# Low parts of sixteen weight blocks: a subtraction on VectorE replaced by a second ScalarE copy and an accumulating SBUF-to-SBUF transfer

## The chip, the cores and the metric

The kernel runs on one core of a Trainium2 chip, as one launch. The metric is device time in microseconds (us). The engines are TensorE (PE in the profile; PEld is its weight load), VectorE (DVE), ScalarE (ACT), GpSimd (POOL) and SyncE (SP, which here only issues DMA transfers). Each runs its own instructions in order and waits for others by semaphores. Sixteen DMA engines move the data of all queues.

## The reference, cut to what matters

One inference step of a decoder layer on 512 prompt positions and 8 x 4 sample positions (544 rows of 1024 channels). A wide input projection feeds three branches (mLSTM, spatial gating, RG-LRU), each is gated, projected and merged, then comes an output projection and a layer norm. The change touches the weights of two of the fifteen parts of the input projection, z_b and u_b:

```python
proj = jnp.einsum('btd,de->bte', x, p['w_in']) + p['b_in']
(q, k, v_a, o_a, z_a, i_pre, f_pre, u_b, v_b, z_b, x_c, z_c,
 g_a, g_b, g_c) = jnp.split(proj, _split_points(), axis=-1)
...
vn = layer_norm(v_b, p['gmlp_ln_g'], p['gmlp_ln_b'])
y_b = chunk_spatial_gate(u_b, vn, p['gmlp_ws'], p['gmlp_bs']) * jax.nn.silu(z_b)
```

All data is float32.

## The kernel before

**Split products.** A float32 product is made from three TensorE products of rounded numbers (type float32r): each operand is split into a high part (the rounded value) and a low part (what is left), and high x high, high x low and low x high are added in PSUM. For x the parts are xh and xl, held in SBUF for the whole run, transposed (8 tiles of 128 channels x 544 rows). For weights they are made block by block.

**Units.** The work on TensorE is a list of tasks, each 128 output columns of one weight matrix: names like zb0 to zb7 and u0 to u7. For a plain task `project` (L414) runs one unit: 8 contraction steps k, each with 3 x 2 products of 128x272 (`products`, L349): first two with (wh, xh), then two with (wh, xl), then two with (wl, xh). So wl is read from the fifth product of a unit on. The task zb0 takes the steps in the order 4 to 7, then 0 to 3. The vb pairs just before zb0 go through `seven` (L360), a scheme with seven products of half blocks.

**Weights.** `load` (L262) fetches raw weights for two neighbouring tasks (256 columns, 1 MB, two SP transfers) into one of two raw buffers. `need` (L274) makes wh and wl of one task from it: ScalarE writes wh = raw, rounded to float32r (L286), then VectorE writes wl = raw - wh (L287). wh and wl have three buffers each. `prep(n+2)` is called at step k = 1 of unit n, so the parts of a unit are made two units ahead. For zb0 and zb1 that call stands inside `seven` of the last vb pair, in its third and fourth part.

**Order.** The program order of TensorE, ScalarE, VectorE and GpSimd is as written; side work (generators: `norm_v`, `mixers`) is put between products by a clock that counts the TensorE work issued so far. Around the first zb units there are also: the restore of eight pieces of xh and xl from DRAM (`restore`, L497, by SP), the loads of the layer-norm rows (L1366, L1367), the transposes and the layer norm of v (`norm_v`, L1361), and `mixers` (L1303), whose affine_select (L1310) and the power of the layer norm (L1354) run on GpSimd. Ahead of each u unit TensorE makes the mix products (`pre_u`, L1286). Results of a unit are taken from PSUM by ScalarE (L758, L759 for zb) and VectorE.

**Accumulating transfers before.** GpSimd issues twenty transfers that add 256 KB of raw weights from DRAM onto SBUF (`block`, L253, with onto), for the tasks that go through `seven`, mostly two in a row: one onto a raw buffer (wr), one onto s3 (shown as s).

Of the kernel before, what the change touches and what calls it, by code (L numbers as in the profile page):

```python
# [11 lines left out]
AF = mybir.ActivationFunctionType  # L12
ALU = mybir.AluOpType
PSUM = bass.MemoryType.PSUM

P = 128
# [25 lines left out]
def kernel(  # L42
# [6 lines left out]
    nc = tc.nc  # L49
    ET = mybir.EngineType  # L50
    ctx.enter_context(tc.manual_schedule(engines={ET.PE, ET.Activation, ET.DVE, ET.Pool}))
    V, A, G, PE = nc.vector, nc.scalar, nc.gpsimd, nc.tensor
# [33 lines left out]
    def f(ap):  # L86
        return ap.bitcast(F32)
# [174 lines left out]
    def load(i):  # L262
        name, w2d, off, c, *_ = tasks[i]
        c0 = off - c * P
        if (id(w2d), c0) not in raws:
            raws[id(w2d), c0] = raw = sp.tile([P, KT, 256], F32, tag="wraw", name=f"wr_{name}", bufs=2)
            for q in range(0, KT, 4):
                nc.sync.dma_start(raw[:, q:q + 4, :], w2d[q * P:(q + 4) * P, c0:c0 + 256].rearrange("(k p) c -> p k c", p=P))
            if name in fast:

                block(raw[:, 0:4, P:2 * P], i, 1, 1, True)
        return raws[id(w2d), c0]

    def need(i, parts=1):  # L274
        if i >= len(tasks) or i in wts:
            return
        name, w2d, off, c, *_ = tasks[i]
        raw = load(i)
        wh = sp.tile([P, KT, P], F32R, tag="wh", name=f"wh_{name}", bufs=3)
        wl = sp.tile([P, KT, P], F32R, tag="wl", name=f"wl_{name}", bufs=3)  # L280
        wts[i] = (wh, wl)
        n = KT // parts
        for q in range(parts):
            ks = slice(q * n, q * n + n)
            src = raw[:, ks, c * P:(c + 1) * P]
            A.activation(wh[:, ks, :], src, AF.Copy)  # L286
            V.tensor_tensor(wl[:, ks, :], src, f(wh[:, ks, :]), op=ALU.subtract)  # L287
            yield
# [48 lines left out]
    def prep(n, whole=True):  # L337
        if n >= len(seq):
            return
        if n not in preps:  # L340
            i, q = seq[n]
            preps[n] = need(i) if q is None else factors(i, q)
        if whole:
            for _ in preps[n]:
                pass
        else:
            next(preps[n], None)
# [189 lines left out]

    def start():
        w0, w1 = need(0, 4), need(1, 4)

        warm = m2("warm")
# [15 lines left out]
        xps[1] = x_rows(1)  # L557
        heat(3)
        w2 = need(2, 2)
        for k in range(KT):  # L560
            if k + 1 < KT:
# [183 lines left out]
    ya, yc, zb, yb = {}, {}, {}, {}  # L745
# [867 lines left out]
```

## Time and profile before

| | us |
|---|---|
| median of 3 runs | 980.22 (977.94 to 981.2) |
| the profiled execution | 978.44 |
| its span, from the first to the last instruction | 976.4 |
| TensorE busy | 959.8 |
| VectorE busy | 613.3 |
| ScalarE busy | 447.9 |
| GpSimd busy | 123.4 |

The profile is of one execution. Its page gives busy times and the chain of work that ended last; the trace behind it answers for a stretch, an engine or a tile. Times within the span count from its start. An instruction line gives its start, its duration, the engine, the line of the kernel, and what it writes and reads (`out<-in`); an x4 merges four like instructions. In brackets stands the idle time of the engine ahead of it and what ended that. "Landing" is the time from a transfer's issue to its completion.

### The profile page before, as it was taken

The page shows a single profiled execution, that of the slowest core. Times are in us where ns is not written, and L with a number is a line of the kernel's source. Part 1 is how long each engine was busy: PE and PEld are TensorE (multiplying, and loading weights), DVE is VectorE, ACT ScalarE, POOL GpSimd, SP SyncE. Part 2 cuts the span into 40 slices and gives each one's busy share as a digit, 9 for nine tenths or more (in the row PEclk, how much of TensorE's full clock was granted, in tenths as well). Part 3 has the DMA queues.
Part 4 walks back from the last instruction along what each step waited for, and adds up shares of the span by engine and source line. Part 5 has one row for each costly group of instructions (what it writes and reads, how often), then busy time and mean ns, then how long its engine had stood idle before and what let it go on. Part 6 is the DMA issues. An engine that isn't in the chain of part 4 may idle for free.

```text
span 976.4 us, 17919 instructions
## 1 busy us (share of the span) xinstructions
PE 959.8 (98%) x7313; PEld 934.2 (96%) x7313; DVE 613.3 (63%) x1033; ACT 447.9 (46%) x747; POOL 123.4 (13%) x230
## 2 busy tenths in 40 slices
PE   9999999999999999999999999999999999999996
PEld 8999999999999999999999999999999999999975
DVE  4665675566567568889987465556677455433456
ACT  4454445445444544889935353334433213322411
POOL 5122101200210120001111111112000000000204
PEclk9999999999999999999999999999999999999999
DMA  9333622541362252332153755557633222430322
GB/s 300 104 63 120 218 66 77 177 149 44 121 217 74 74 165 85 98 97 78 59 131 90 143 136 129 119 137 161 179 118 114 87 92 76 142 113 34 103 66 102
DMA packets 120113, 113.64 MB, mean 116 GB/s; under 512 B 6094, under 2 KB 113464, under 8 KB 120032
## 3 DMA queue, kind: packets, MB, share of 16 engines
q1 hardware_dynamic: 107936, 106.31, 34.8%
q0 software_dynamic: 11456, 5.55, 4.9%
q8 instruction: 57, 0.93, 0.4%
q10 hardware_dynamic: 640, 0.66, 0.2%
q14 instruction: 24, 0.20, 0.1%
HBM read 99.38 MB, written 13.11 MB: 115 GB/s over the span
## 4 chain that ended last, share of the span: by engine, by line
PE 89%; DVE 5%; ACT 2%; DMA 1%; issue 1%; POOL 0%; POOLq 0%; DVEq 0%; ACTq 0%
PE out L103 5%; PE ps_v L103 5%; PE ps_zc L103 5%; PE ps_u L103 5%; PE ps_z L103 5%; PE ps_q L103 5%; PE ps_zb L103 5%; PE ps_xc L103 5%; PE ps_pb L103 5%; PE ps_o L103 5%; PE ps_k L103 5%; PE ps_pc L103 5%; PE ps_gb L103 5%; PE ps_pa L103 2%; PE px_gc L103 2%; PE sc L103 2%
## 5 line engine op out<-in xcount | busy, mean ns | idle before, releaser
L993 DVE SCALAR_TENSOR_TENSOR c<-c,bc,cs 128x512 f32<-128x512 f32 x32 | 23.9, 747 | 36.2 <-PE cs L103 35.8
L975 POOL TENSOR_SCALAR wvm<-wvt,bm 96x256 fp32r<-96x256 f32 x32 | 31.5, 987 | 87.4 <-PE cs L103 87.4
L103 PE MATMUL ps_v<-xh,wh_v 128*128 128x272 f32 x128 | 28.4, 305 | 0.0
L972 ACT ACTIVATE c0h<-c 128x512 fp32r<-128x512 f32 x32 | 20.0, 625 | 17.2 <-DMA c<-in_state_mlstm_c_dram 8.8
L103 PE MATMUL ps_v<-xh,wl_v 128*128 128x272 f32 x128 | 27.4, 296 | 0.0
L103 PE MATMUL ps_u<-xh,wh_u 128*128 128x272 f32 x128 | 27.3, 295 | 0.0
L103 PE MATMUL ps_q<-xh,wh_q 128*128 128x272 f32 x128 | 27.3, 294 | 0.0
L103 PE MATMUL ps_v<-xl,wh_v 128*128 128x272 f32 x128 | 27.3, 295 | 0.0
L103 PE MATMUL ps_zc<-xh,wh_zc 128*128 128x272 f32 x128 | 27.2, 295 | 0.0
L103 PE MATMUL ps_o<-xl,wh_o 128*128 128x272 f32 x128 | 27.2, 293 | 0.0
L103 PE MATMUL ps_zc<-xl,wh_zc 128*128 128x272 f32 x128 | 27.1, 294 | 0.0
L103 PE MATMUL ps_zc<-xh,wl_zc 128*128 128x272 f32 x128 | 27.0, 293 | 0.0
L103 PE MATMUL ps_zb<-xh,wl_zb 128*128 128x272 f32 x128 | 27.0, 292 | 0.0
L103 PE MATMUL ps_z<-xh,wl_z 128*128 128x272 f32 x128 | 26.9, 291 | 0.0
L103 PE MATMUL ps_o<-xh,wl_o 128*128 128x272 f32 x128 | 26.8, 291 | 0.0
L103 PE MATMUL ps_z<-xh,wh_z 128*128 128x272 f32 x128 | 26.7, 290 | 0.0
L103 PE MATMUL ps_q<-xl,wh_q 128*128 128x272 f32 x128 | 26.7, 289 | 0.0
L103 PE MATMUL ps_q<-xh,wl_q 128*128 128x272 f32 x128 | 26.7, 290 | 0.0
L103 PE MATMUL ps_zb<-xl,wh_zb 128*128 128x272 f32 x128 | 26.6, 289 | 0.0
L103 PE MATMUL ps_zb<-xh,wh_zb 128*128 128x272 f32 x128 | 26.6, 289 | 0.0
L103 PE MATMUL ps_xc<-xl,wh_xc 128*128 128x272 f32 x128 | 26.6, 289 | 0.0
L103 PE MATMUL ps_k<-xh,wl_k 128*128 128x272 f32 x128 | 26.6, 289 | 0.0
(905 smaller groups left out, 3471.3 us busy)
## 6 DMA issues: line engine op xcount, KB each, us to landing
c<-in_state_mlstm_c_dram SPq DMA_DIRECT2D x32, 256.0 KB
out_dram<-c SPq DMA_DIRECT2D x32, 256.0 KB
wr_q<-in_w_in_dram SPq DMA_DIRECT2D x8, 512.0 KB
wr_k<-in_w_in_dram SPq DMA_DIRECT2D x8, 512.0 KB
wr_o<-in_w_in_dram SPq DMA_DIRECT2D x8, 512.0 KB
wr_z<-in_w_in_dram SPq DMA_DIRECT2D x8, 512.0 KB
wr_xc<-in_w_in_dram SPq DMA_DIRECT2D x8, 512.0 KB
wr_zc<-in_w_in_dram SPq DMA_DIRECT2D x8, 512.0 KB
```

Of the source, the lines that this page charges most:

```text
L103: PE.matmul(out, a, b, start=start, stop=stop, skip_group_check=more)
L972: A.activation(hi[:, :512], t_[:, :512], AF.Copy)
L975: G.tensor_scalar(wvm, f(wvs), bm[:, b:b + 1], None, op0=ALU.mult)
L993: V.scalar_tensor_tensor(t_[:, :512], t_[:, :512], inter[:, DS * b + DS - 1:DS * b + DS], ps, op0=ALU.mult, op1=ALU.add)
```

## The change

For the tasks zb0 to zb7 and u0 to u7 the low part is made in another way. ScalarE writes wh as before, for all 8 steps in one instruction, and then writes wl = -raw, rounded in the same way, that is -wh. Then GpSimd issues a transfer from SBUF to SBUF that adds the raw weights onto wl (512 KB, in pieces of 128 numbers, since raw holds the columns of two tasks). wl is then raw - wh. VectorE has no part in it, and the raw buffer is read last by that transfer. All other tasks stay as they were.

```diff
@@ -279,6 +279,14 @@
         wh = sp.tile([P, KT, P], F32R, tag="wh", name=f"wh_{name}", bufs=3)
         wl = sp.tile([P, KT, P], F32R, tag="wl", name=f"wl_{name}", bufs=3)
         wts[i] = (wh, wl)
+        if name[:-1] in ("zb", "u"):
+
+            src = raw[:, :, c * P:(c + 1) * P]
+            A.activation(wh, src, AF.Copy)
+            A.activation(wl, src, AF.Copy, scale=-1.0)
+            nc.gpsimd.dma_start(f(wl), src, accum_op=ALU.add)
+            yield
+            return
         n = KT // parts
         for q in range(parts):
             ks = slice(q * n, q * n + n)
```

## Rows read from the trace of the kernel before

**Rows 1.** The page: busy time, share of the span and number of instructions of each engine; then the chain that ended last, its shares of the span by engine.
```profile
PE 959.8 (98%) x7313; PEld 934.2 (96%) x7313; DVE 613.3 (63%) x1033; ACT 447.9 (46%) x747; POOL 123.4 (13%) x230
...
PE 89%; DVE 5%; ACT 2%; DMA 1%; issue 1%; POOL 0%; POOLq 0%; DVEq 0%; ACTq 0%
```

**Rows 2.** The waits of TensorE over the whole span, longest first: who waited for whom, us in total, times, the longest.
```profile
PE px_ga L103 <- ACT gta L370: 1.5, 1, 1.5
```

**Rows 3.** Busy time by windows, the stretch of the zb units and that of the u units: window, its length, busy us of each engine with the number of instructions, the granted clock of TensorE, the share of the DMA engines, GB/s.
```profile
702.10:760.00 57.90, 57.90 (x467) 57.18 (x467) 39.57 (x63) 20.14 (x28) 3.24 (x6) 1.00 0.44 137
760.00:820.00 60.00, 60.00 (x464) 58.19 (x464) 31.63 (x47) 12.69 (x16) 0.00 (x0) 1.00 0.24 80
```

**Rows 4.** The chain that ended last, in order of time, around the first zb unit: start, us, what.
```profile
700.42 1.23 DVE wl_zb L287
701.65 0.36 DVE vbt L382
...
702.06 1.77 PE px_vb L103 x12
...
704.49 0.51 PE ps_zb L103 x4
```

**Rows 5.** The timeline of TensorE: the last product ahead of the gap at 702, and the first two products that read wl of zb0.
```profile
701.65 0.29 PE L103 MATMUL py_vb<-xh,wl_vb 128*128 128x272 f32 x1
...
705.62 0.50 PE L103 MATMUL ps_zb<-xh,wl_zb 128*128 128x272 f32 x2
```

**Rows 6.** The instructions that read the raw weights of zb: number, duration in ns (least, median, most), first and last start, shapes.
```profile
L286 ACT ACTIVATE wh_zb<-wr_zb x8: 1049/1058/1062, 699.3 to 741.4; 128x1024 fp32r<-128x1024 f32 x8
L287 DVE TENSOR_TENSOR wl_zb<-wr_zb,wh_zb x8: 1216/1222/1227, 700.4 to 743.7; 128x1024 fp32r<-128x1024 f32 x8
```

**Rows 7.** The same view for the low parts of u on VectorE.
```profile
L287 DVE TENSOR_TENSOR wl_u<-wr_u,wh_u x8: 1206/1216/1225, 750.6 to 800.4; 128x1024 fp32r<-128x1024 f32 x8
```

**Rows 8.** The timeline of ScalarE: wh of zb0 and zb1, the evacuation of zb0, wh of zb4, the evacuations of zb2 and zb3, wh of u0.
```profile
699.34 1.05 ACT L286 ACTIVATE wh_zb<-wr_zb 128x1024 fp32r<-128x1024 f32 x1
701.85 1.06 ACT L286 ACTIVATE wh_zb<-wr_zb 128x1024 fp32r<-128x1024 f32 x1 [1.46 <-PE py_vb L103]
...
711.87 0.72 ACT L758 ACTIVATE t_zb<-ps_zb,vh__167 128x544 f32<-128x544 f32 x1 [3.01 <-PE ps_zb L103]
...
721.59 1.05 ACT L286 ACTIVATE wh_zb<-wr_zb 128x1024 fp32r<-128x1024 f32 x1
727.28 0.71 ACT L758 ACTIVATE t_zb<-ps_zb,vh__167 128x544 f32<-128x544 f32 x1 [4.64 <-PE ps_zb L103]
...
733.31 0.71 ACT L758 ACTIVATE t_zb<-ps_zb,vh__167 128x544 f32<-128x544 f32 x1 [3.76 <-PE ps_zb L103]
...
748.32 1.06 ACT L286 ACTIVATE wh_u<-wr_u 128x1024 fp32r<-128x1024 f32 x1
```

**Rows 9.** The timeline of GpSimd: two pairs of accumulating loads of 256 KB each; the duration is that of the issue.
```profile
503.36 1.40 POOL L258 DMA_DIRECT2D wr_ga<-in_w_in_dram  x1 [9.57 <-DVE tl L462]
504.22 1.88 POOL L258 DMA_DIRECT2D s<-in_w_in_dram  x1
...
533.16 1.27 POOL L258 DMA_DIRECT2D wr_ga<-in_w_in_dram  x1 [27.06 <-DMA wr_ga<-in_w_in_dram]
533.91 1.83 POOL L258 DMA_DIRECT2D s<-in_w_in_dram  x1
```

**Rows 10.** The transfers issued from 503 to 513 us: number, KB each, us from issue to landing.
```profile
wr_ga<-in_w_in_dram POOLq DMA_DIRECT2D x1, 256.0 KB, 4.8
s<-in_w_in_dram POOLq DMA_DIRECT2D x1, 256.0 KB, 5.9
```

**Rows 11.** The timeline of SP's queue near the two pairs (x2: two transfers of 512 KB); SP issues nothing else from 502 to 512 us.
```profile
509.75 1.62 SPq L268 DMA_DIRECT2D wr_pa<-in_w_proj_a_dram  x2
...
533.95 0.92 SPq L268 DMA_DIRECT2D wr_pa<-in_w_proj_a_dram  x2
```

**Rows 12.** The transfers that GpSimd issued from 533 to 545 us, columns as in rows 10.
```profile
wr_ga<-in_w_in_dram POOLq DMA_DIRECT2D x1, 256.0 KB, 6.4
s<-in_w_in_dram POOLq DMA_DIRECT2D x1, 256.0 KB, 8.6
```

**Rows 13.** The three small transfers (at most 8.5 KB) that GpSimd issues from SBUF to hrows in DRAM, near 53 us.
```profile
DMA to landing us min/median/max: 1.6/1.7/1.7
```

**Rows 14.** Busy time by windows around the first zb unit, columns as in rows 3.
```profile
700.00:705.00 5.00, 4.88 (x40) 4.59 (x39) 3.55 (x5) 2.42 (x4) 0.00 (x0) 1.00 1.03 333
705.00:710.00 5.00, 5.00 (x43) 4.95 (x42) 3.25 (x6) 1.66 (x3) 1.05 (x2) 1.00 0.95 278
```

**Rows 15.** The timeline of GpSimd near the first zb unit: the affine_select of mixers and the first power of the layer norm.
```profile
688.87 1.18 POOL L1310 TENSOR_SCALAR_AFFINE_SELECT wsr<-wsr 128x512 f32<-128x512 f32 x1
707.72 0.57 POOL L1354 TENSOR_TENSOR brsv<-brsv,mhalf 128x1 f32<-128x1 f32 x1 [17.68 <-DVE brsv L1353]
```

**Rows 16.** The timeline of SP's queue: the first loads of raw weights for u (four transfers, from the first issue to the end of the last).
```profile
732.04 13.78 SPq L268 DMA_DIRECT2D wr_u<-in_w_in_dram  x4
```

**Rows 17.** Busy time by windows at the end of the span, columns as in rows 3: the last slice with TensorE work, and two slices after it.
```profile
967.00:968.00 1.00, 0.93 (x8) 0.73 (x7) 0.78 (x3) 0.00 (x0) 1.00 (x1) 1.00 0.13 53
...
972.00:973.00 1.00, 0.00 (x0) 0.00 (x0) 0.65 (x1) 0.00 (x0) 0.88 (x2) 1.00 0.88 325
973.00:974.00 1.00, 0.00 (x0) 0.00 (x0) 0.00 (x0) 0.00 (x0) 0.00 (x0) 0.55 0.85 314
```

## The prediction

> **What bounds the kernel now.** I read the page first: TensorE is busy 98% of the span and carries 89% of the chain that ended last [rows 1]. Then the waits of TensorE alone: the longest in the whole span is 1.5 us [rows 2]. Then the stretch that the change touches, cut by windows: from 702.1 us, where the zb units begin, to 820, where the u units end, TensorE is busy 117.9 of 117.9 us, VectorE 71.2 and ScalarE 32.8 [rows 3]. So nothing that VectorE does in this stretch is waited for by TensorE. Time can only be won where TensorE has a gap, and any new gap is added in full, since the chain runs on through TensorE almost to the end [rows 1]. The one gap near the change lies just ahead of it: TensorE ends the py_vb products that start at 701.65 and goes on at 702.06, after VectorE wrote wl_zb (from 700.42) and then the vbt addition that the next product waits for [rows 4, 5]. That is some 0.3 us.
>
> **What is removed.** Sixteen subtractions of 128x1024 on VectorE, 8 of 1.22 us for zb and 8 of 1.22 for u [rows 6, 7], 19.5 us of VectorE in all. They lie beside TensorE work that has no gap [rows 3], so they are worth nothing, except the 0.3 us gap at 702.06, where wl_zb stands in front of the vbt addition [rows 4]. I count that as a gain only where the new transfer is in time, because else the later wait swallows it.
>
> **What is added on ScalarE.** Sixteen more copies of 128x1024. ScalarE's copy of the same shape takes 1.06 us [rows 6]; I take the same with a scale of -1. Together 17 us on an engine that is busy 32.8 of 117.9 us [rows 3]. Queued behind each are the evacuations of the running unit: behind the copy at 721.59 the next is the tanh at 727.28, ahead of which ScalarE sat idle for 4.64 us until TensorE was done [rows 8], so the second copy goes into that idle time. Without it each would put an evacuation off by 1.06 us, and TensorE only if that held up a PSUM bank.
>
> **What is added on the path to the matmul.** The low part was ready 2.3 us after ScalarE began (1.06 plus 1.22). Now it is ready when ScalarE has written twice (2.1 us), GpSimd has issued the transfer, and 512 KB have been added and have landed. TensorE needs wl four matmuls after a unit's first, 0.5 us into it [rows 4]. What the trace lacks is an accumulating transfer of 512 KB from SBUF. The nearest rows are GpSimd's accumulating loads of 256 KB from DRAM, which come in pairs, so that a pair moves the 512 KB in the same 512-byte pieces. Alone on the engines (the next SP load is issued at 509.75), the pair issued at 503.36 and 504.22 landed 5.9 us after the second issue, at 510.1: 6.8 us for both [rows 9 to 11]. With a load of 1 MB beside it (SP, from 533.95) the pair of 533.16 and 533.91 landed 8.6 us after the second issue, at 542.5: 9.35 us [rows 9, 11, 12]. The lower bound is a single 256 KB, 4.8 us [rows 10], or less if reading SBUF is quicker than reading DRAM: small transfers out of SBUF land after 1.7 us [rows 13]. The upper bound I set at 11.5 us, the price beside the load plus once more what the load added (9.35 - 6.8 = 2.55).
>
> **Steady state: hidden.** The tightest unit is zb4: its wh is written from 721.59, the unit before it ends at 733.31, and wl is wanted 0.5 us later, 12.2 us after the start [rows 4, 8]. Two copies and the hand-over take 2.2, which leaves 10.0 us for issue and landing, against 6.8 alone and 9.35 beside a load. It fits with 0.7 to 3 us to spare, and for the u units, which begin with the 1.3 us of mix products, with more. Cost nothing; the cover is TensorE's own work, and what it costs if gone is a rival below.
>
> **zb0: not hidden.** zb0 and zb1 are prepared late, inside the last fast pair. ScalarE writes wh_zb0 from 699.34 (the earliest that the buffer is free), wl_zb0 to 701.5, and TensorE wants wl_zb0 at 705.62 [rows 5, 8]: 4.1 us for a transfer that takes 6.8 alone. And it is not alone: the DMA engines are busy all the time from 700 to 710 (shares of 1.03 and 0.95) with the eight restored x pieces, a raw load and the layer-norm rows [rows 14]. Nearest is therefore the pair with a load beside it, 9.35; I take 9.0, since one instruction stands in place of two that were issued 0.75 apart [rows 9]. Landing at 710.5, a gap of 4.9 us (2.7 by the price alone, 7.4 by the upper bound).
>
> The Trainium skill ("DMA: Bandwidth & Descriptors", section "Anatomy of one DMA — SWDGE (gpsimd) path") gives such a transfer as 2.0 us plus its bytes over 436 GB/s. By that it would be an estimated 3.2 us, would land before 705.62, and the sum would be 0. The trace disagrees: for 256 KB the page makes it 2.6 us, and the row has 4.8 without anything beside it [rows 10].
>
> **zb1 and the queues.** wl_zb1 is written by 704.0 (from 701.85) and its transfer follows zb0's on the same queue; half of the pair's price after 710.5 it lands near 715. It was wanted at 712.4 (zb0's end at 711.87 and 0.5), now 4.9 later, 717.3 [rows 8]: no second gap. On GpSimd the two issues, each waiting for ScalarE, are put ahead of the affine_select that ran at 688.87 and the power of the first layer norm at 707.72; GpSimd is through with them near 707 (704.0 plus the 2.7 that a pair's issue takes), and the affine_select takes 1.2, so the power slips by some 0.2 us, on VectorE's side only [rows 9, 15]. On SP a raw buffer now comes free with the landing, up to 7.7 us later than with the subtraction: the loads that went out from 732.04 go from 739.7, and ScalarE wants them at 748.32; 1 MB at the 333 GB/s of the busy stretch takes 3.2 [rows 8, 14, 16]. Behind them on SP wait only stores and w_out loads. Nothing on any of these paths reaches TensorE.
>
> **Sum.** 0 from VectorE, 0 from steady state, +4.9 at zb0: the profiled execution of 978.44 us (span 976.4) becomes 983.3. That run lies 1.8 under the median of the timed ones, 980.22; taking the middle between the two, 979.3, as the base, the forecast for a median is 984.2. 0.3%, about what a measurement of this kernel can tell from no change, is 2.9 us.
>
> **Rivals.**
> (A) Forecast: one gap of 3 to 7.4 us at zb0, 982 to 987. For it: 4.1 us of cover, against 6.8 at the least for these bytes.
> (B) The other side, not slower: reading SBUF is quick, and the transfer takes 7.0 or less in spite of the traffic, so that the gap is 0 to 2.9 us; 979.0 (with the 0.3 us gap closed) to 982.2, the middle 980.7. It decides at 4.1 us of landing for no loss at all and at 7.0 for the 0.3%. For it: the 1.7 us rows and the 6.8; against it: the full DMA engines at 700 to 710. Of its chance 0.06 is for no gap at all. (The formula of the Trainium skill's page, the estimate above, would be that end.)
> (C) The transfer takes over 10 us in steady state too. At 12 us the units zb4 to u0 each lack up to 2 us; a gap in one unit gives the next one as much more time, so about every second one pays, some 5 us, and zb0 has a gap of 7.9: 992. Against it: from 720 on the traffic is thin, and 9.35 is the worst pair.
> (D) The gap makes TensorE's clock fall. At the end of the span TensorE stops at about 967.9; its granted clock is still 1.00 up to 973 and 0.55 in the slice after, on its way from the level of 2.4 GHz to that of 1.2 [rows 17]. So some 5 us without work brought it down there, and my gap is about as long. No row prices the way back; as an estimate, running at half speed for another 5 us loses 2.5: 986.7.
> (E) Faster by over 0.3%: there is no 3 us gap in TensorE's work that the change could close.
>
> **How the numbers follow.** A 0.50, B 0.28, C 0.08, D 0.12, E 0.02. Faster 0.02, within 0.3% 0.28, slower 0.70. The likeliest is A, 984.2. The range leaves out the better half of B and most of C: 980.3 to 990.
>
> **What would show it.** In the profile after: VectorE short of sixteen subtractions; a wait of TensorE in ps_zb on a DMA that writes wl_zb, one, of about 5 us, between 705 and 711; no wait of TensorE on wl_zb from zb2 on, nor on wl_u; landings of the new transfers near 9 us for zb0 and 7 later. I am wrong if the first landing is under 7 us or if later units wait too, which would mean that the rows of loads from DRAM don't price a transfer inside SBUF.

## The result and the profile after

| | before | after |
|---|---|---|
| median, runs side by side | 979.08 us (4 runs, 976.03 to 981.2) | 991.31 us (4 runs, 985.46 to 992.73) |
| the profiled execution | 978.44 | 985.46 |
| its span | 976.4 | 983.8 |
| VectorE busy | 613.3 | 594.3 |
| ScalarE busy | 447.9 | 462.9 |
| GpSimd busy | 123.4 | 148.7 |

The changed kernel is slower: ratio 1.0113, 95% interval [1.0084, 1.0141], some 11 us. Two repetitions gave 1.0117 [1.0096, 1.0138] and 1.0114 [1.0084, 1.0144]. The forecast was 984.2, the range ended at 990.0.

The page's first part, after, beside [rows 1]: VectorE has 16 instructions and 19 us less, ScalarE 16 more, and TensorE about the same work in a longer span.

```profile
PE 958.3 (97%) x7313; PEld 932.2 (95%) x7313; DVE 594.3 (60%) x1017; ACT 462.9 (47%) x763; POOL 148.7 (15%) x246
```

The waits of TensorE (us in total, times, longest). Before, the longest was the 1.5 us of [rows 2]; now one stands far above it, and there is a small new one at the first u unit. No other unit waits for its low part.

```profile
PE ps_zb L103 <- DMA wl_zb<-wr_zb: 8.9, 1, 8.9
PE px_ga L103 <- ACT gta L378: 1.5, 1, 1.5
...
PE ps_u L103 <- DMA wl_u<-wr_u: 0.2, 1, 0.2
```

The timeline of TensorE around the big wait. The transposes of v end at 701.8, then nothing runs until the first product with wl_zb0. It takes 0.82 us where it took 0.50 [rows 5], and the pairs behind it take 0.65 until 714, then 0.41 again.

```profile
699.59 0.38 PE L107 MATMUL nnps<-ident,nn 128*36 128x128 f32 x2
...
700.75 1.04 PE L107 MATMUL vt<-ident,vbt 128*128 128x128 f32 x8
710.67 0.82 PE L103 MATMUL ps_zb<-xh,wl_zb 128*128 128x272 f32 x2 [8.88 <-DMA wl_zb<-wr_zb]
711.29 0.65 PE L103 MATMUL ps_zb<-xh,wh_zb 128*128 128x272 f32 x2
...
715.09 0.41 PE L103 MATMUL ps_zb<-xl,wh_zb 128*128 128x272 f32 x2
```

Windows over the same stretch (columns as in rows 3). TensorE stands still for all of 705:710 while the DMA engines are full; the granted clock is 0.50 there and 0.52 in the next slice, the level of 1.2 GHz, although TensorE is at work again from 710.67. In cuts of one us the clock is 1.00 to 704, 0.78 in the next, 0.50 until 714, 0.60, then 1.00.

```profile
700.00:705.00 5.00, 1.79 (x16) 1.53 (x14) 2.08 (x5) 2.15 (x5) 2.77 (x3) 0.96 0.92 208
705.00:710.00 5.00, 0.00 (x0) 0.00 (x0) 2.56 (x4) 0.89 (x1) 2.12 (x2) 0.50 1.27 266
710.00:715.00 5.00, 4.33 (x20) 4.09 (x21) 0.44 (x1) 0.00 (x0) 0.00 (x0) 0.52 1.46 186
715.00:720.00 5.00, 5.00 (x43) 5.00 (x42) 0.00 (x0) 1.79 (x3) 0.00 (x0) 1.00 0.65 154
```

The chain that ended last (start, us, what). The path leaves TensorE twice, both times to an accumulating transfer: zb0's, 12.5 us, and u0's, 10.7. Behind zb0's stand 14 products that take 3.54 us; before, at full clock, the same 14 took 1.75, as the second fence shows, which is the chain of before at the same place.

```profile
698.11 12.51 DMA wl_zb<-wr_zb
710.63 0.04 issue
710.67 3.54 PE ps_zb L103 x14
714.21 0.79 PE lvps L107 x4
715.00 4.78 PE ps_zb L103 x38
...
757.62 10.66 DMA wl_u<-wr_u
```
```profile
705.87 1.75 PE ps_zb L103 x14
707.62 0.44 PE lvps L107 x4
708.06 4.77 PE ps_zb L103 x38
```

**How to compare the spans.** From run to run of the same code TensorE comes to this stretch earlier or later: its first product after the vb pairs (nnps) starts between 699.6 and 706.9 us in the profiled executions of all kernels here, whose code is alike up to the last vb pair. So I compare the time from there to the end of the span. Before it starts at 703.7 (the row below), which leaves 272.7 us; after at 699.6, which leaves 284.2: +11.5. The profiled execution of after had an early start; that goes with its 985.46 being the lowest of its four.

```profile
703.67 0.38 PE L107 MATMUL nnps<-ident,nn 128*36 128x128 f32 x2
```

The 11.5 are made up as follows: the wait at zb0, 8.9; the slower 14 products and 4 transposes behind it, 3.54 - 1.75 and 0.79 - 0.44, together 2.1 (of which 0.3 comes with any wait here: behind waits of 1.4 and 2.0 us the 14 took 2.02 at full clock, experiments 5 and 8); the wait at u0, 0.2. That is 11.2; 0.3 I can't place. In the two repetitions the waits at zb0 were 9.3 and 9.2, and the rests 284.0 and 285.5.

### The profile page after: what moved, and what is told of

Same layout as the page of the kernel before. It is cut to its first block, busy times and chain, and to the rows that moved or that the text cites. A ratio compares the mean times of both kernels' runs of the same rounds, so it can differ in the third digit from the quotient of the medians.

```text
span 983.8 us, 17968 instructions
## 1 busy us (share of the span) xinstructions
PE 958.3 (97%) x7313; PEld 932.2 (95%) x7313; DVE 594.3 (60%) x1017; ACT 462.9 (47%) x763; POOL 148.7 (15%) x246
## 4 chain that ended last, share of the span: by engine, by line
PE 89%; DVE 5%; DMA 3%; ACT 2%; issue 1%; POOL 0%; ACTq 0%; POOLq 0%; DVEq 0%
PE out L103 5%; PE ps_v L103 5%; PE ps_u L103 5%; PE ps_z L103 5%; PE ps_q L103 5%; PE ps_zc L103 5%; PE ps_xc L103 5%; PE ps_pb L103 5%; PE ps_o L103 5%; PE ps_k L103 5%; PE ps_pc L103 5%; PE ps_gb L103 5%; PE ps_zb L103 4%; PE ps_pa L103 2%; PE px_vb L103 2%; PE px_gc L103 2%
## 5 line engine op out<-in xcount | busy, mean ns | idle before, releaser
L103 PEld LDWEIGHTS ps_zb<-xh,wl_zb 128*128 128x128 f32 x128 | 20.6, 194 | 9.1 <-DMA wl_zb<-wr_zb 9.1
L103 PE MATMUL ps_u<-xh,wl_u 128*128 128x272 f32 x128 | 26.6, 289 | 0.2 <-DMA wl_u<-wr_u 0.2
L103 PE MATMUL ps_gb<-xh,wh_gb 128*128 128x272 f32 x128 | 26.5, 288 | 0.0
```

Source lines behind the costliest of these rows:

```text
L103: PE.matmul(out, a, b, start=start, stop=stop, skip_group_check=more)
```

## The experiments

Three theories. **T**: zb0's transfer has too little time, and loads that SP put on the DMA engines shortly before hold it up; the loss lies there alone. **R**: the new transfers hold each other up, or wait in GpSimd's own queue. **S**: a part of the loss is spread, over the later units or the copies on ScalarE. Within T there is the question what the clock adds.

**1. zb0 made by VectorE as before, all else changed.**

```diff
-        if name[:-1] in ("zb", "u"):
+        if name[:-1] in ("zb", "u") and name != "zb0":
```

> zb0's low part is made by VectorE as before, zb1 to zb7 and u0 to u7 by copy and transfer. Theory T (traffic): zb0's transfer took 12.5 us because SP's transfers (restored x pieces, raw weights, layer-norm rows) were on the DMA engines at the same time. Then zb1's, issued some 2.4 us later into the same traffic, still takes 10 to 12 us, TensorE wants it some 8 us after its issue, and a gap of 2 to 4 us stands at zb1; time 2 to 5 us over the kernel before. Theory R (own queue): the transfers of zb0, zb1 and zb2 slowed each other on GpSimd's one queue. Then zb1's, now the first, lands after 6 to 8 us, TensorE has no gap, and the time is that of before within 2 us.

982.51 us against 980.39, ratio 1.0030 [1.0014, 1.0046]. The waits of TensorE have one on a low part, and it is in zb1; the chain shows its transfer in the second fence:

```profile
PE ps_zb L103 <- DMA wl_zb<-wr_zb: 2.8, 1, 2.8
```
```profile
707.55 10.78 DMA wl_zb<-wr_zb
```

The granted clock stays 1.00 throughout. zb1's transfer is now the first of the new kind, with none ahead of it on GpSimd's queue, and still takes 10.8 us, where R expected 6 to 8. So R doesn't carry the loss (experiment 8 tries it once more). In the changed kernel zb1's transfer took 13.0 us and TensorE didn't wait for it; that zb0's gap gave it the time is how I read it.

**2. zb0 and zb1 made by VectorE.** The condition is `name not in ("zb0", "zb1")`.

> zb0's and zb1's low parts are made by VectorE as before, zb2 to zb7 and u0 to u7 by copy and transfer. Theories T and R: no wait of TensorE on wl over 0.3 us, time within 0.3% of the kernel before. Rival S (spread): fourteen of the sixteen copies and transfers remain, so if part of the 12 us is paid at each of them, 8 us or more of loss remain.

981.08 us against 980.39, ratio 1.0009 [1.0000, 1.0019]. No wait is left in the zb units; one of 0.8 us at u0 stands, which neither T nor R expected. So nearly the whole loss is in the first two units, and S falls but for u0.

**3. The restore left out.** `restore()` isn't called, which takes 1.1 MB of loads out of the stretch; zb0 and the units behind it then read other values in these columns.

> The changed kernel without the eight transfers that bring the middle pieces of x back from DRAM (1.1 MB, about 3 us of the DMA engines at the 360 GB/s they ran at); the products of zb0 and later then read other values in these columns, so that part of the computation is left out. Theory T: zb0's transfer lands after 9 to 10 us, not 12.5, and TensorE's gap at zb0 is 5.5 to 6.5 us, not 8.9. Theory R: landing 12 or more, gap 8.5 to 9.5.

984.96 us in one run. The transfer of zb0 lands after 8.15 us, the wait is 4.5; both lie under what T expected (9 to 10, and 5.5 to 6.5). The chain, and then the windows:

```profile
701.90 8.15 DMA wl_zb<-wr_zb
710.09 3.19 PE ps_zb L103 x14
```
```profile
705.00:710.00 5.00, 0.58 (x6) 0.34 (x4) 4.18 (x8) 1.72 (x2) 4.01 (x5) 1.00 1.36 215
710.00:715.00 5.00, 4.91 (x27) 4.67 (x28) 0.30 (x1) 0.59 (x1) 0.13 (x1) 0.66 1.37 181
```

Less traffic, quicker landing, as T says. The clock fell all the same, but later: 1.00 through the slice of the wait and 0.66 in the slice after it.

**4. Both copies, no transfer.** The line with the transfer is taken out, so that wl stays -wh.

> The changed kernel with both ScalarE copies, but without the sixteen transfers that add the raw weights, so that wl holds the negated high part. Theories T and R: TensorE has no wait at zb or u, and the time is that of the kernel before or up to 0.5 us less (the short gap ahead of the first zb unit closes). Rival S, as far as the copies on ScalarE carry it: slower by 2 us or more.

979.77 us against 980.39, ratio 0.9997 [0.9986, 1.0008], and the time from nnps to the end is 272.7, as before. The ScalarE copies cost nothing that can be measured, and the sixteen subtractions that VectorE no longer does gain nothing. The loss is the transfer's.

**5. The changed kernel again, and with TensorE kept at work during the wait** (`turned` is zb0, `first` its first step).

```diff
+            if n == 1 and tasks[i][0] == turned and k == first:
+                hot = aux("hot")
+                for _ in range(64):
+                    PE.matmul(hot[:, :HT], wh[:, k, :], vh[k][:, 0:HT], start=True, stop=True)
```

> The changed kernel once more, beside the two below. Theory T: TensorE waits once for wl_zb of zb0, 8 to 10 us, and at most 1 us for wl_u of u0; slower than before by 9 to 13 us.

> The changed kernel, with 64 more products of 128x272 (8 us) on TensorE, into a PSUM bank that nobody reads, between the fourth product of zb0 and the first that waits for wl. If the half clock behind the gap costs the 2 us that the first fourteen products after it take longer, then the granted clock stays at 1.00 from 700 to 716 us, the rest of the gap is 1 to 2 us, and the time is 2 us less than the changed kernel's. If those products were slow for another reason, such as the weights still arriving, the time stays the same.

The changed kernel: 991.67 against 980.87, ratio 1.0117. With the 64 products, whose result nobody reads: 989.44, ratio 1.0094 [1.0071, 1.0117]. The transfer takes 13.1 us, no less than without them. The timeline of TensorE, and then the chain:

```profile
705.12 8.28 PE L370 MATMUL hot<-xh,wh_zb 128*128 128x272 f32 x64
714.81 0.52 PE L103 MATMUL ps_zb<-xh,wl_zb 128*128 128x272 f32 x2 [1.41 <-DMA wl_zb<-wr_zb]
```
```profile
701.64 13.12 DMA wl_zb<-wr_zb
714.81 2.02 PE ps_zb L103 x14
```

The granted clock is 1.00 in every slice from 700 to 720, and the 14 products take 2.02 us in place of 3.33 to 3.54. The medians differ by 2.2 us, with intervals that overlap a little, and from nnps to the end it is 283.2 us beside 284.0 and 285.5 of the repetitions: the rows show the mechanism; the size is some 1 to 2 us, which the times alone don't show clear of noise.

**6. zb0's transfer in two halves of 256 KB**, the steps that are used first ahead. Run twice.

```diff
-            nc.gpsimd.dma_start(f(wl), src, accum_op=ALU.add)
+            for hf in ((1, 0) if name == turned else ()):
+                ks = slice(4 * hf, 4 * hf + 4)
+                nc.gpsimd.dma_start(f(wl[:, ks, :]), raw[:, ks, c * P:(c + 1) * P], accum_op=ALU.add)
+            if name != turned:
+                nc.gpsimd.dma_start(f(wl), src, accum_op=ALU.add)
```

> The changed kernel, with zb0's transfer issued as two of 256 KB, the half for the steps 4 to 7, which TensorE takes first, ahead of the other. Theory T (the DMA engines share their time between SP's and GpSimd's queues): the first half lands after 7 to 8 us and the second after 12 to 13; a gap of 3 to 4.5 us at the first half and 1 to 3 at the second, little or no half clock; 3 to 5 us less than the changed kernel. If instead GpSimd's transfer makes no headway until SP's traffic is through, the first half lands after 10 us or more, and less than 2.5 us are gained.

> The kernel of e6_halves once more, since its times (985.6, some 6 us less than the changed kernel's) and its profiled execution (a wait of 6.2 us at zb0, the granted clock 0.50 to 0.53 in 705:715, 284 us to within 1.4 from the first product after the vb pairs to the end) do not go together. If the times are right: 984 to 989, and a profile with a wait at zb0 of 4 to 6 us. If the profile is: 988 to 992. Both would mean that the first half, 256 KB, lands later than the 4.8 us that such a transfer took by itself.

> The changed kernel beside it on the same chip: 990 to 993, a wait of 8.5 to 9.5 us at zb0 and a landing of its transfer after 12 to 13 us, as in the two profiles so far.

First 985.6, ratio 1.0062 [1.0039, 1.0084], then 987.49, ratio 1.0089 [1.0068, 1.0110], beside 990.72 of the changed kernel, 1.0114. Both profiles have a wait of 6.1 to 6.2 us, and 282.8 and 281.2 us from nnps to the end, where the changed kernel has 284.0 to 285.5. So the halves save some 3 us, though the intervals of the second run and its neighbour overlap, and the 6 of the first times were partly chance. The first half alone, in the chain of the second run:

```profile
699.73 9.85 DMA wl_zb<-wr_zb
709.63 3.28 PE ps_zb L103 x14
```

256 KB take 9.85 us here; the accumulating load of 256 KB took 4.8 with nothing beside it [rows 10]. Halving the bytes saves only a quarter of the time. What I expected from T, 7 to 8 us for the first half and a wait of 3 to 4.5, did not come; the result lies near the other case's 10 us, in which the transfer makes no headway until SP's loads are through. (The second half stood on the same queue behind the first, so the 9.85 aren't for 256 KB by themselves.)

**7. zb0, zb1 and u0 by VectorE.** The condition is `name not in ("zb0", "zb1", "u0")`.

> zb0, zb1 and u0 get their low parts from VectorE as before, the other thirteen by copy and transfer. Theory T, in which the waits of TensorE are the whole loss: the 0.8 us wait at u0 that is left without zb0 and zb1 is gone, no wait on wl is over 0.3 us, and the ratio to the kernel before is 1.000, 0.0005 to 0.001 under that of the kernel with u0 changed. If something else of the change costs time, the ratio stays at 1.001 or more. It is not faster than before in either case, since VectorE's time is not waited for.

978.64 us against 980.71, ratio 0.9982 [0.9968, 0.9996]. TensorE waits for no low part, and the time from nnps to the end is 272.6, beside 272.7 before: in the stretch that the change touches nothing is gained. The 0.2% are not from there, and I don't count them as a gain of this version.

**8. Restore left out and the layer-norm rows not loaded** (filled with ones by VectorE). `restore()` is left out as in experiment 3; the diff shows the rest.

```diff
-            nc.sync.dma_start(a[:, :512], gln_g[0:1, hf * 512:hf * 512 + 512].to_broadcast([P, 512]))
-            nc.sync.dma_start(b[:, :512], gln_b[0:1, hf * 512:hf * 512 + 512].to_broadcast([P, 512]))
+            V.memset(a[:, :512], 1.0)
+            V.memset(b[:, :512], 1.0)
```

> The changed kernel without the restored x pieces (as in the third run) and without the four loads of layer-norm rows (1 MB), in whose place VectorE writes ones; what depends on them is left out of the computation. Half a MB of raw weights is all that SP still moves beside zb0's transfer. Theory T: landing after 6 to 7 us (5.7 is what the transfers take with nothing beside them), gap at zb0 2 to 3 us, clock at 1.00. If the first transfers are slow because of their place on GpSimd's queue (three follow one another within 8 us), landing stays at 8 us or more.

982.89 us in one run. The transfer lands after 5.66 us, TensorE waits 2.0, and the clock stays at 1.00. zb1's transfer is issued on the same queue 2.35 us behind zb0's, as in the changed kernel, so that the queue isn't what held zb0's up there. The chain:

```profile
704.46 5.66 DMA wl_zb<-wr_zb
710.16 2.03 PE ps_zb L103 x14
```

**The runs together.** The transfers by queue, from the issue of zb0's transfer to its landing (packets, MB, the time of the packets as a share of 16 engines' time; q1 has SP's transfers, q0 GpSimd's): first the changed kernel, then the third experiment, then the last.

```profile
q1 hardware_dynamic: 1953, 2.38, 67.7%
q0 software_dynamic: 1293, 0.65, 41.3%
```
```profile
q0 software_dynamic: 1442, 0.73, 71.3%
q1 hardware_dynamic: 830, 1.28, 50.1%
```
```profile
q0 software_dynamic: 1190, 0.60, 84.8%
q1 hardware_dynamic: 225, 0.20, 10.4%
```

| kernel | SP's transfers meanwhile (q1) | landing of zb0 | wait | landing - wait |
|---|---|---|---|---|
| changed, third time (experiment 6) | 2.46 MB | 12.84 us | 9.2 | 3.64 |
| changed, again (experiment 5) | 2.44 MB | 12.95 | 9.3 | 3.65 |
| changed | 2.38 MB | 12.51 | 8.9 | 3.6 |
| restore left out | 1.28 MB | 8.15 | 4.5 | 3.65 |
| both left out | 0.20 MB | 5.66 | 2.0 | 3.66 |

The last column is the cover: the same in every run, so the wait is the landing less 3.65 us, and the landing grows with the megabytes, though not evenly: 2.3 us per MB from the last row to the one above it, 4.0 from there to the changed kernel. (A longer landing also counts some more of SP's transfers.)

Cutting the landing shows where the time goes. In the first 5.0 us after the issue (698.11:703.11) GpSimd's queue moves nothing in the changed kernel, while SP's moves 1.27 MB; in the third experiment it moves nothing for 3.0 us (701.90:704.90); in the last, with hardly anything beside it, for 2.0 (704.46:706.46). The three lines are all that ran on queues in these windows:

```profile
q1 hardware_dynamic: 1281, 1.27, 91.8%
```
```profile
q1 hardware_dynamic: 580, 0.90, 97.7%
```
```profile
q1 hardware_dynamic: 177, 0.16, 23.6%
```

Behind that late start the transfer goes slowly as long as SP still has loads: 0.45 MB in the 5 us of 705:710 (first fence, changed kernel), where it moves 0.36 in 2 us by itself (second, 707:709 of the last experiment).

```profile
q0 software_dynamic: 893, 0.45, 71.3%
q1 hardware_dynamic: 532, 0.88, 55.5%
```
```profile
q0 software_dynamic: 712, 0.36, 144.7%
```

So of the 6.9 us between the landings of the last experiment and of the changed kernel some 3 to 4 are a later start, and the rest a slower passage. The shares are no budget to add up: with one queue alone the packets' time reaches 144.7%, and in the changed kernel the two queues' shares make 109%.

## Why the prediction was wrong

**Right: where.** One gap, at zb0; nothing from VectorE (experiment 4); nothing from the copies on ScalarE (4); no wait in zb1 to zb7 nor in u1 to u7; TensorE waits nowhere for the power or affine_select on GpSimd. Rival A's mechanism is what happened. Rival C did not: landings with thin traffic are shorter than I took, not longer. GpSimd's transfers from 715 to 756:

```profile
DMA to landing us min/median/max: 5.7/5.7/8.4
```

Against 10.0 us of cover that is ample. (zb1's and zb2's, issued into the traffic before, took 13.0 and 10.8.) B's premise, that a transfer inside SBUF is quick, is half true: 5.7 us against the 6.8 of the pair [rows 9, 10], but even so zb0 would wait 2.0 (experiment 8). The Trainium skill ("DMA: Bandwidth & Descriptors", section "Anatomy of one DMA — SWDGE (gpsimd) path") would give an estimated 3.2 us for these bytes; the trace has 5.7 for the accumulating transfer with nothing beside it.

**Wrong: the landing of zb0, "Nearest is therefore the pair with a load beside it, 9.35; I take 9.0".** It measured 12.5 to 13.0, above even the bound of 11.5 (which by its own sum, 9.35 plus 2.55, should have read 11.9). The pair of [rows 12] had 1 MB of SP's loads beside it; zb0's transfer had 2.4, and I had read the windows that showed it: 333 and 278 GB/s over 700 to 710 [rows 14] are 3.1 MB in 10 us. I used them to say that the engines were busy and not to count. By my own two prices a megabyte adds 2.55 us; 2.4 of them on 6.8 make 12.9. That this comes so near is partly luck: by themselves these bytes land after 5.7, not 6.8, and the megabytes cost 2.3 us at first and 4.0 later, since the transfer first starts late, which I had no term for, and then shares the engines. This step is 3.5 to 4.0 us of the error. The smaller part of the same step: the cover was 3.65 us, not 4.1, since between the end of ScalarE's copy (697.7 in the changed kernel) and the issue on GpSimd (698.11) lie some 0.4; I had 0.1 for this in the steady state and nothing here.

**Wrong: D as a rival beside A.** The clock is no other way in which it could go but a consequence of a gap of A's size. With waits of 2.0 and 2.8 us the clock stayed at 1.00 in all slices; with 4.5 it was 0.66 in the slice behind; with 8.9 it was 0.50 in the slice of the wait and 0.52 in the one behind, and the 14 products behind the wait took twice their time. From [rows 17] I took some 5 us between TensorE's stop and the fall. Here TensorE stopped at 701.8 and the clock was down to 0.78 from 704 to 705. Price, over the 2.02 us that the 14 products take behind a wait at full clock: 1.9 us in the profiled run (1.52 and 0.35 for the transposes), 1.3 and 2.8 in the repetitions (14 products in 3.33 and 3.54, in the latter also 38 in 5.64 in place of 4.77, and the transposes in 0.85). D's estimate, 2.5, was fair; it should have been added to the forecast.

**Wrong in a small matter: "Nothing on any of these paths reaches TensorE".** SP's load of raw weights for u2 waits for the raw buffer, which now comes free with the landing of zb7's transfer. That is at 756.5 (its issue at 750.8 and the 5.7 above); the load goes out at 756.59, one us before u0's transfer is issued at 757.62, and the loads of w_out follow from 757.56. With these on the engines u0's landing takes 10.7 us in place of 5.7, against a cover of 10.4.

```profile
756.59 0.92 SPq L268 DMA_DIRECT2D wr_u<-in_w_in_dram  x2
```

The wait was 0.2 to 0.8 us in all runs that had the transfer at u0 but that of experiment 1, where the landing took 10.3 us and TensorE didn't wait, and it is gone in experiment 7. I had followed the late loads only to whoever reads them, and not to whoever is on the DMA engines beside them.

**The sum, corrected.** Landing 12.5 to 13.0, less 3.65 of cover, is a gap of 8.9 to 9.3 in place of 4.9; 0.3 for starting again and 1.3 to 2.8 for the clock; 0.2 to 0.4 at u0: 11 to 13 us, beside the 11 of the ratios.

**What stays open.** Why the start of the stretch differs by up to 7 us from run to run of the same code. What keeps GpSimd's transfer from starting while SP's loads run: the windows show that it does not start, and not by what. What decides when the clock falls: a wait of 2.8 us left it alone (experiment 1), in experiment 3 it fell only when the wait was over, and in the first repetition it was already 0.61 in 708:709, with TensorE's last product before the wait in 706:707. A kernel that makes zb0's and zb1's parts earlier, with more buffers for wh and wl, was not run.

## What to carry to other kernels

Price a transfer by what else is on the DMA engines from its issue to its landing, in bytes, and not by the nearest transfer of its size: here 512 KB took 5.7 us alone, 8.15 beside 1.3 MB and 12.5 to 13.0 beside 2.4 MB, and half of them still 9.85. Taking work off an engine that isn't waited for (19.5 us of VectorE) is worth nothing, while the longer path that it is moved to must fit into every place, the first unit of a phase above all, where the lead of two units doesn't exist yet. And a gap in TensorE's work has a second price behind it, its clock: to a wait of 8.9 us came another 1.9.

## What the hardware showed that I had not expected

- **An accumulating transfer takes the DMA engines longer per byte.** In the changed kernel's rows above SP's 2.38 MB have 67.7% of the engines' time and GpSimd's 0.65 MB 41.3%: 0.28 and 0.64 per MB, a factor of 2.2. The small pieces aren't the reason: below are a plain load in the same 512-byte pieces (SP's of 527.43 in the kernel before, in a window of 2.4 us), which comes to 4.0 us of engine time per MB, and zb3's transfer (722.88:728.6, a window of 5.72 us), with 8.1. The Trainium skill ("Collectives: The Full Stack", section "The bandwidth ceiling: the fold count and why AG ≠ RS ≠ AR") says of the reductions in collectives that the add needs two source reads, and gives 1.93 for the ratio of two collectives; the factor here agrees in kind.

```profile
q1 hardware_dynamic: 528, 0.26, 42.9%
```
```profile
q0 software_dynamic: 1040, 0.52, 73.3%
```

- **One issue of 512 KB takes GpSimd 1.55 to 1.60 us**, as in the row below, where a pair of 256 KB took 2.6 to 2.7 from the first issue to the end of the second [rows 9].

```profile
698.11 1.56 POOL L287 DMA_DIRECT2D wl_zb<-wr_zb  x1 [11.57 <-ACT wl_zb L286]
```

- **The clock doesn't come back with the work.** TensorE was at work again from 710.67, and the granted clock was 0.50 until 714; with the 64 products of experiment 5 it never fell, though they did nothing useful. In experiment 3 it even fell after the wait: TensorE was at work from 710.09, and the clock was 1.00 to 710, then 0.77 and 0.50 in the next slices of one us.
